# Feed-forward products transposed by VectorE blocks and DRAM transfers instead of by TensorE, with selective forcing of tasks

## The chip, the cores and the metric

One core of a Trainium2 chip runs the kernel. The metric is the device time of one execution in microseconds (us). Three timed executions of the kernel before took 2844.18, 2844.20 and 2846.04 us, so the median is 2844.2 us. The rows further down come from one more execution, taken by the hardware profiler.

## What is computed

A trunk of two blocks works on an input `x` of 256 tokens and 2048 channels in fp32. The first block has two layers, each with a mixer and a feed-forward part; the second block is a state-space and pooling layer. The part that the change touches is the feed-forward, with 5632 hidden channels:

```
def swiglu(u, w_gate, w_up, w_down):
    return (jax.nn.silu(u @ w_gate) * (u @ w_up)) @ w_down

def first_block(x, ...):
    h = x
    for layer in range(DEPTH):                       # 2
        u = rms_norm(h, mix_norm_pre[layer])
        u = even_mixer(u, ...) if layer % 2 == 0 else odd_mixer(u, ...)
        h = h + rms_norm(u, mix_norm_post[layer])
        u = swiglu(rms_norm(h, ffn_norm_pre[layer]), w_gate, w_up, w_down)
        h = h + rms_norm(u, ffn_norm_post[layer])
    return h
```

## The kernel before

Every large product runs as **units**. A unit is one block of 128 rows of a weight matrix by 512 of its columns, for both halves (t = 0, 1) of the 256 tokens. To hold fp32 accuracy each operand is split into a high and a low part, so a unit is six matmuls: `wh` by `uh`, `wl` by `uh` and `wh` by `ul` (L329 to L331), twice. A **panel** is 512 output columns, in the feed-forward's gate and up products 16 units long.

Weights come in **chunks** of two units. `fetch` (L225) issues a 512 KB transfer per chunk into `wr` on SyncE's queue (SP), which has five buffers. `split` then lets ScalarE (ACT) write `wh` and VectorE (DVE) write `wl` (L363 and L364) into four buffers each, three chunks ahead of TensorE (PE).

The Python program writes the instructions of all engines in one order by hand, and each engine works through its own instructions in that order. `order` lays out the units; between units it hangs in **hooks** (norms, transposes of `h`) and **tasks**. A task is a generator: each `yield n` lets n units pass before its next step, and `tick`, after every unit, steps at most three tasks that are due. `drain(sel)` forces the tasks in `sel` to their end at one spot. In doing so it steps every task that is alive, whether it is in `sel` or not.

One drain stands at unit 15 of the first product: it forces the first norm (`rms`) because the product's result needs its factor `rs`. Alive at that spot are also `load_gains(1, ...)`, which issues five small transfers to `gsrc`, yields 30 units, and then transposes `gsrc` on PE (L157); and `ab_proj`, which loads `abw` and yields 7.

In the feed-forward (`ffn`) the 11 pairs of gate and up panels come in three parts of 4, 4 and 3, each followed by the down product over that part's columns. `gate_evac` makes `sg`, and `up_evac` multiplies it with the up result into `mid` (L483), one 128x512 tile for each t. The down product needs `mid` with hidden channels on the partitions, so a task, four or five units later, transposes it on PE in four 128x128 pieces (`transposes`, L467) into the PSUM tile `aux`, and ACT and DVE split that into `mh` and `ml` (L360 and L361). A drain at unit 10 of the down product (unit 6 in the last part) sees to it that this has been issued. The down product runs four panels, each over all 16 (or 12) K blocks in order. Layer 0's feed-forward also carries the task `ssm_prep`, which prepares tables of the second block with DVE work and transfers of its own.

Of the kernel before, what the change touches and what calls it, by code (L numbers as in the profile page):

```python
# [10 lines left out]
F32 = mybir.dt.float32  # L11
# [4 lines left out]
OP = mybir.AluOpType  # L16
# [4 lines left out]
P = 128  # L21
# [76 lines left out]
def trunk(ctx: ExitStack, tc: tile.TileContext, I, out):  # L98
    nc = tc.nc
    PE, ACT, DVE, POOL = nc.tensor, nc.scalar, nc.vector, nc.gpsimd  # L100
# [9 lines left out]
    drp = ctx.enter_context(tc.tile_pool(name="drp", bufs=1, space=DRAM))  # L110
# [4 lines left out]
    def big(name, dt=F32R):  # L115
        return bp.tile([P, KT, S], dt, name=name, tag="b16")

    def aux(name="aux"):
        return psa.tile([P, 512], F32, name=name, tag="aux")

    def t4(name, n=1024, dt=F32):
        return t4p.tile([P, 1024], dt, name=name, tag="t4")[:, :n]

    def t2(name, n=512, dt=F32):
        return t2p.tile([P, 512], dt, name=name, tag="t2")[:, :n]
# [34 lines left out]
    units, chunks, tasks, now = [], [], [], [0]  # L160
    phs, due = [], []

    def phase(norm=True, begin=None):
        phs.append(dict(a=len(units), norm=norm, begin=begin))

    def gemm(src, wap, kts, panels, evac, kc=2, gi=None, late=None):

        steps = [(j, 0, len(kts)) for j in range(len(panels))]
        if late:
            steps[:2] = [(0, 0, late), (1, 0, late), (0, late, len(kts)), (1, late, len(kts))]  # L170
        pss = [{} for _ in panels]
        for j, g0, g1 in steps:
            c0, c1 = panels[j]
            n = c1 - c0
            for g in range(g0, g1, kc):
                ks = kts[g:g + kc]
                chunks.append((wap, ks, c0, c1, gi))
                for i, k in enumerate(ks):
                    units.append(dict(chunk=len(chunks) - 1, i=i, k=k, src=src, n=n, j=j, pn=pss[j],
                                      first=g + i == 0, last=g + i == len(kts) - 1, evac=evac,  # L180
                                      before=[], after=[]))

    def spawn(gen, gap=3, delay=1):
        tasks.append(Task(gen, gap, now[0] + delay))
        return tasks[-1]
# [15 lines left out]
        due.append((now[0] + n, f))  # L201

    def drain(sel):
        while any(not x.done for x in sel):
            for d in due:
                d[1]()
            due.clear()
            moved = [x.step(now[0]) for x in list(tasks)]
            tasks[:] = [x for x in tasks if not x.done]
            assert any(moved)  # L210

    W, nf = {}, [0]
    LA, SA, HEAD, TAIL, EXTRA, CAP = 4, 3, 12, 8, 3, 3
# [37 lines left out]
    def order():  # L251
# [3 lines left out]
        for pi, (p, end) in enumerate(zip(phs, ends)):  # L255
# [19 lines left out]
            if nm.norm:  # L275
                us[KT - 1]["before"].append(lambda n=nm: drain([n.task]))
# [72 lines left out]
    def square_sum(src, ss, t, j):  # L349
        junk = sp.tile([P, 512], BF16, name="junk", tag="junk", bufs=1)  # L350
        ACT.activation(junk[:, :src.shape[-1]], src, AF.Square, accum_out=ss[:, t, j:j + 1])  # L351
# [4 lines left out]
    st = dict(upd=lambda t, c: None, post=lambda t: None)  # L356

    def split_evac(hi, lo, src, gain=None):
        if gain is None:
            ACT.activation(hi, src, AF.Copy)  # L360
            DVE.tensor_sub(lo, src, hi.bitcast(F32))  # L361
        else:
            ACT.activation(hi, src, AF.Copy, scale=gain)  # L363
            DVE.scalar_tensor_tensor(lo, src, gain, hi.bitcast(F32), OP.mult, OP.subtract)  # L364
# [56 lines left out]
    def cut(x, j):  # L421
        return x[j // 2][:, (j % 2) * 512:(j % 2 + 1) * 512]
# [21 lines left out]
    def cols(n, base=0, w=512):  # L444
        return [(base + i * w, base + (i + 1) * w) for i in range(n)]
# [13 lines left out]
    def h_src(k):  # L459
        a, b = st["mh"][k // 8]  # L460
        return a[:, k % 8, :], b[:, k % 8, :]

    def transposes(src):

        p4 = aux()
        for i in range(4):
            PE.transpose(p4[:, i * P:(i + 1) * P], src[:, i * P:(i + 1) * P], ident)  # L467
        return p4

    def ffn(layer, gi, begin=None, end=None):  # L470
        phase(begin=begin)
        wg, wu, wd = I["ffn_w_gate"][layer], I["ffn_w_up"][layer], I["ffn_w_down"][layer]
        sg = {}

        def gate_evac(j, t, src):
            s = t2("sg")
            ACT.activation(s, src, AF.Silu, scale=st["rs"][:, t:t + 1])
            sg[t] = s

        def up_evac(p0):  # L480
            def f(j, t, src):
                m = t2("mid")
                DVE.scalar_tensor_tensor(m, src, st["rs"][:, t:t + 1], sg[t], OP.mult, OP.mult)  # L483
                mh, ml = st["m"]

                def go():
                    p4 = transposes(m)
                    k = p0 * 4
                    v = p4.rearrange("p (k s) -> p k s", k=4)
                    split_evac(mh[:, k:k + 4, t * P:(t + 1) * P], ml[:, k:k + 4, t * P:(t + 1) * P], v)  # L490
                    yield
                st["mid_tasks"].append(spawn(go(), delay=4 + t))
            return f

        def down_evac(first, last):
            def f(j, t, src):
                acc = cut(st["acc"][t], j)
                if first:
                    ACT.activation(acc, src, AF.Copy)
                    return  # L500
                DVE.tensor_add(acc, src, acc)
                if last:
                    square_sum(acc, st["ssp"], t, j)
                    if j < 3:
                        POOL.tensor_mul(acc, acc, cut(st["wpost"], j))  # L505
                    elif t == 0:
                        post_end(True)
            return f

        for pi, (p0, p1) in enumerate(PARTS):  # L510
            b = len(units)
            for p in range(p0, p1):
                gemm(u_src, wg, KTS, [(p * 512, (p + 1) * 512)], gate_evac, gi=gi)
                gemm(u_src, wu, KTS, [(p * 512, (p + 1) * 512)], up_evac(p - p0), gi=gi)
            units[b]["before"].append(lambda: st.update(m=(big("mh"), big("ml")), mid_tasks=[]))
            c = len(units)
            kts = list(range((p1 - p0) * 4))
            gemm(m_src, wd[p0 * 512:p1 * 512, :], kts, cols(4), down_evac(pi == 0, pi == 2))
            units[c + len(kts) - 6]["before"].append(lambda: drain(st["mid_tasks"]))
            if pi == 0:  # L520
                units[c]["before"].append(post_begin)
            if pi == 2:
                units[c]["before"].append(lambda: load_post(I["ffn_norm_post"][layer]))
            if pi == 2 and end:
                units[c]["before"].append(end)
# [1072 lines left out]

    mix0()
    ffn(0, 1, prep, lambda: drain([ssm["task"]]))  # L1600
    mix1()
    ffn(1, 3)
# [28 lines left out]
```

## Time and profile before

| what | value |
|---|---|
| median of three timed executions | 2844.2 us |
| the profiled execution | 2845.48 us |
| its span, first to last instruction | 2843.7 us |
| mean granted clock of TensorE | 0.996 |
| busy share PE, DVE, ACT, GpSimd (POOL) | 99%, 62%, 53%, 7% |
| moved by DMA | 552.25 MB, mean 194 GB/s |

An engine's busy share counts the time in which at least one of its instructions runs. Matmuls overlap (each takes some 0.39 us, while one starts every 0.23 us), so PE's real pace is read from the starts of its instructions. PEld is PE's weight load, which overlaps its matmuls. Idle time is put down to what ended it.

### The profile page before, as it was taken

To read this page: it belongs to the slowest core of one execution; us is meant where nothing else is said; L and a number is where in the kernel's file an instruction comes from. 1 tells how busy PE (TensorE), PEld (TensorE's weight loads), DVE (VectorE), ACT (ScalarE), POOL (GpSimd) and SP (SyncE) were. 2 spreads that over 40 slices of the span, in tenths; PEclk is the share of its full clock that TensorE was granted. 3 is DMA by queue.
4 is the path that set the end of the run, shared out by engine and by line. 5 is a ranking of instruction groups with operands and counts; after the bars stand their busy time and mean duration, and the time that the engine had idled before them with its cause. 6 is when DMAs were issued, how large, how long until landed. Compare 5 with 4: busy or idle time off the path is not lost.

```text
span 2843.7 us, 36948 instructions
## 1 busy us (share of the span) xinstructions
PE 2812.8 (99%) x13599; PEld 2312.8 (81%) x13599; DVE 1771.2 (62%) x2703; ACT 1504.9 (53%) x2380; POOL 192.6 (7%) x290
## 2 busy tenths in 40 slices
PE   7999999999999999999999999999999999999998
PEld 5888888888888778878888888888888887878887
DVE  4777766678666666566666565545555556575555
ACT  4666554655555445555555465545544545555444
POOL 0150410000000011000000000000000001100000
PEclk9999999999999999999999999999999999999999
DMA  6564746576767677755556656666656665875654
GB/s 204 170 183 139 196 151 198 162 209 204 219 212 210 213 212 235 228 172 182 171 170 186 190 179 192 188 193 191 190 191 191 189 207 185 298 249 177 194 192 144
DMA packets 305670, 552.25 MB, mean 194 GB/s; under 512 B 43032, under 2 KB 52816, under 8 KB 305488
## 3 DMA queue, kind: packets, MB, share of 16 engines
q1 hardware_dynamic: 295232, 515.52, 59.8%
q0 software_dynamic: 10224, 34.35, 3.8%
q8 instruction: 107, 1.75, 0.3%
q14 instruction: 75, 0.61, 0.1%
q10 hardware_dynamic: 32, 0.01, 0.0%
HBM read 532.24 MB, written 21.76 MB: 195 GB/s over the span
## 4 chain that ended last, share of the span: by engine, by line
PE 95%; DVE 2%; DMA 1%; ACT 1%; issue 0%; SPq 0%; ACTq 0%; POOLq 0%; POOL 0%; DVEq 0%
PE mm L329 30%; PE mm L331 29%; PE mm L330 29%; PE aux L467 1%; DVE wl L364 1%; PE aux L380 1%; ACT wh L363 0%; PE aux L1359 0%; DMA wr<-in_ev_w_in_dram 0%; DMA wr<-in_ffn_w_up_dram 0%; DMA b<-in_b_im_dram 0%; PE aux L1449 0%; PE aux L1218 0%; PE aux L556 0%; PE aux L582 0%
## 5 line engine op out<-in xcount | busy, mean ns | idle before, releaser
L364 DVE SCALAR_TENSOR_TENSOR wl<-wr,gT,wh 128x512 fp32r<-128x512 f32 x1248 | 884.6, 752 | 545.9 <-ACT wh L363 544.7
L363 ACT ACTIVATE wh<-wr,gT 128x512 fp32r<-128x512 f32 x1248 | 829.8, 716 | 536.8 <-PE mm L331 495.9
L329 PE MATMUL mm<-wh,uh 128*128 128x512 f32 (+1 forms) x2656 | 1058.5, 399 | 2.6 <-ACT uh L360 1.3
L331 PE MATMUL mm<-wh,ul 128*128 128x512 f32 (+1 forms) x2656 | 1032.5, 389 | 1.6 <-DVE ul L361 1.6
L330 PE MATMUL mm<-wl,uh 128*128 128x512 f32 (+1 forms) x2656 | 1030.2, 388 | 1.1 <-DVE wl L242 0.9
L242 DVE TENSOR_TENSOR wl<-wr,wh 128x1024 fp32r<-128x1024 f32 x324 | 401.3, 1243 | 355.6 <-ACT wh L241 355.2
L331 PEld LDWEIGHTS mm<-wh,ul 128*128 128x128 f32 x2656 | 499.6, 188 | 111.0 <-DVE ul L361 6.9
L329 PEld LDWEIGHTS mm<-wh,uh 128*128 128x128 f32 x2656 | 500.4, 188 | 104.8 <-issue 5.7
L330 PEld LDWEIGHTS mm<-wl,uh 128*128 128x128 f32 x2656 | 500.9, 189 | 97.5 <-DVE wl L364 2.1
L241 ACT ACTIVATE wh<-wr 128x1024 fp32r<-128x1024 f32 x324 | 342.5, 1059 | 398.9 <-PE mm L331 389.8
L329 PE MATMUL mm<-wh,mh 128*128 128x512 f32 x832 | 326.7, 393 | 0.0
L331 PE MATMUL mm<-wh,ml 128*128 128x512 f32 x832 | 324.0, 389 | 0.0
L330 PE MATMUL mm<-wl,mh 128*128 128x512 f32 x832 | 323.8, 389 | 0.0
L329 PEld LDWEIGHTS mm<-wh,mh 128*128 128x128 f32 x832 | 156.2, 188 | 32.8 <-issue 1.4
L331 PEld LDWEIGHTS mm<-wh,ml 128*128 128x128 f32 x832 | 156.2, 188 | 32.7
L330 PEld LDWEIGHTS mm<-wl,mh 128*128 128x128 f32 x832 | 156.3, 188 | 31.5
L505 POOL TENSOR_TENSOR acc<-acc,wpost 128x512 f32<-128x512 f32 x12 | 15.3, 1300 | 789.5 <-ACT junk L351 789.5
L360 ACT ACTIVATE uh<-aux 128x512 fp32r<-128x512 f32 x48 | 28.6, 595 | 63.5 <-PE aux L380 63.5
L360 ACT ACTIVATE mh<-aux 128x512 fp32r<-128x512 f32 (+1 forms) x60 | 32.5, 542 | 55.4 <-PE aux L467 39.1
L361 DVE TENSOR_TENSOR ul<-aux,uh 128x512 fp32r<-128x512 f32 x48 | 32.7, 689 | 41.0 <-ACT uh L360 40.8
L361 DVE TENSOR_TENSOR ml<-aux,mh 128x512 fp32r<-128x512 f32 (+1 forms) x60 | 37.1, 619 | 32.9 <-ACT mh L360 32.1
L347 POOL TENSOR_TENSOR rp<-ms,half 128x1 f32<-128x1 f32 x8 | 6.7, 840 | 471.8 <-DVE ms L346 471.8
(445 smaller groups left out, 2033.1 us busy)
## 6 DMA issues: line engine op xcount, KB each, us to landing
wr<-in_ffn_w_gate_dram SPq DMA_DIRECT2D x176, 512.0 KB, 4.4
wr<-in_ffn_w_up_dram SPq DMA_DIRECT2D x176, 512.0 KB, 4.2
wr<-in_ffn_w_down_dram SPq DMA_DIRECT2D x176, 512.0 KB, 4.5
wr<-in_ev_w_in_dram SPq DMA_DIRECT2D x112, 512.0 KB, 3.9
wr<-in_od_w_in_dram SPq DMA_DIRECT2D x96, 512.0 KB, 3.7
wr<-in_w_in_dram SPq DMA_DIRECT2D x64, 512.0 KB, 4.9
wr<-in_ev_w_out_dram SPq DMA_DIRECT2D x32, 512.0 KB, 4.0
wr<-in_od_w_out_dram SPq DMA_DIRECT2D x32, 512.0 KB, 4.5
```

Of the source, the lines that this page charges most:

```text
L241: ACT.activation(hi, r[:, k:k + m, :], AF.Copy)
L242: DVE.tensor_sub(lo, r[:, k:k + m, :], hi.bitcast(F32))
L329: PE.matmul(o, a, wh, start=u["first"], stop=False)
L330: PE.matmul(o, a, wl, start=False, stop=False)
L331: PE.matmul(o, b, wh, start=False, stop=u["last"])
L360: ACT.activation(hi, src, AF.Copy)
L361: DVE.tensor_sub(lo, src, hi.bitcast(F32))
L363: ACT.activation(hi, src, AF.Copy, scale=gain)
L364: DVE.scalar_tensor_tensor(lo, src, gain, hi.bitcast(F32), OP.mult, OP.subtract)
L380: PE.transpose(p4[:, i * P:(i + 1) * P], h[:, t, k * P:(k + 1) * P], ident)
L467: PE.transpose(p4[:, i * P:(i + 1) * P], src[:, i * P:(i + 1) * P], ident)
L505: POOL.tensor_mul(acc, acc, cut(st["wpost"], j))
```

## The change

Three things change.

- `drain` steps only the tasks that were asked for. The others are stepped, and things set for later are done, only if none of the asked ones can move.
- The products of both token halves go into one tile `mid` of 128x1024. One task per panel pair replaces two. It transposes 32x32 blocks with two DVE instructions into `ty` (`turn`), writes `ty` to a DRAM tile `td` with one transfer of 512 KB (`away`), reads it back into `tz` with four transfers of 128 KB, each to 32 partitions and in runs of 128 numbers, which puts the blocks into their places (`back`), and splits `tz` into `mh` and `ml`. Between these steps pass 2, 4, 5 and 1 units.
- The down product starts its first two panels without the last four K blocks: panels 0 and 1 run over the others, then both over the last four (`late`). The drains move along: all but the last task at the old spot, the last one at unit 22 (14 in the last part).

```
     def drain(sel):
+
         while any(not x.done for x in sel):
-            for d in due:
-                d[1]()
-            due.clear()
-            moved = [x.step(now[0]) for x in list(tasks)]
+            moved = [x.step(now[0]) for x in list(tasks) if x in sel]
+            if not any(moved):
+                for d in due:
+                    d[1]()
+                due.clear()
+                moved = [x.step(now[0]) for x in list(tasks)]
+                assert any(moved)
             tasks[:] = [x for x in tasks if not x.done]
-            assert any(moved)
...
+    def turn(x):
+        n, w = x.shape[1:]
+        y = t4("ty", n * w)
+        for t in range(n):
+            DVE.transpose(y[:, t * w:(t + 1) * w], x[:, t, :].rearrange("p (k b j) -> p b k j", b=4, j=32))
+        return y.rearrange("p (t x) -> p t x", t=n)
+
+    def away(y):
+        d = drp.tile([P, 2, 512], F32, name="td", tag="td", bufs=4)
+        nc.sync.dma_start(d, y)
+        return d
+
+    def back(z, d):
+        n, w = d.shape[1:]
+        for b in range(4):
+            nc.sync.dma_start(z[32 * b:32 * b + 32].rearrange("j (t a) x -> j t a x", t=n),
+                              d.rearrange("(a j) t (b x) -> j t a b x", a=4, b=4)[:, :, :, b])
...
             def f(j, t, src):
-                m = t2("mid")
-                DVE.scalar_tensor_tensor(m, src, st["rs"][:, t:t + 1], sg[t], OP.mult, OP.mult)
+                if t == 0:
+                    st["mid"] = t4("mid").rearrange("p (t c) -> p t c", t=2)
+                m = st["mid"]
+                DVE.scalar_tensor_tensor(m[:, t, :], src, st["rs"][:, t:t + 1], sg[t], OP.mult, OP.mult)
+                if t == 0:
+                    return
                 mh, ml = st["m"]
 
                 def go():
-                    p4 = transposes(m)
+                    y = turn(m)
+                    yield 2
+                    d = away(y)
+                    yield 4
+                    z = t4("tz").rearrange("p (a x) -> p a x", a=8)
+                    back(z, d)
+                    yield 5
                     k = p0 * 4
-                    v = p4.rearrange("p (k s) -> p k s", k=4)
-                    split_evac(mh[:, k:k + 4, t * P:(t + 1) * P], ml[:, k:k + 4, t * P:(t + 1) * P], v)
-                    yield
-                st["mid_tasks"].append(spawn(go(), delay=4 + t))
+                    for t in range(2):
+                        split_evac(*[x[:, k:k + 4, t * P:(t + 1) * P].rearrange("p k (a i) -> p k a i", a=4)
+                                     for x in (mh, ml)], z[:, 4 * t:4 * t + 4].rearrange("p a (k i) -> p k a i", k=4))
+                        yield 1
+                st["mid_tasks"].append(spawn(go(), delay=1))
...
-            gemm(m_src, wd[p0 * 512:p1 * 512, :], kts, cols(4), down_evac(pi == 0, pi == 2))
-            units[c + len(kts) - 6]["before"].append(lambda: drain(st["mid_tasks"]))
+            gemm(m_src, wd[p0 * 512:p1 * 512, :], kts, cols(4), down_evac(pi == 0, pi == 2), late=len(kts) - 4)
+            units[c + 2 * len(kts) - 10]["before"].append(lambda: drain(st["mid_tasks"]))
+            units[c + len(kts) - 6]["before"].append(lambda: drain(st["mid_tasks"][:-1]))
```

Two places show what moves. In the changed kernel the lines up to `drain` keep their numbers, those behind it stand 3 lines lower, and those behind the feed-forward 35 lines lower (L329 is now L332, L364 is L367, L1017 is L1052).

**The drain at unit 15 of the first product.** On PE, before:

```order
L330 MATMUL mm<-wl,uh 128x512
L331 MATMUL mm<-wh,ul 128x512
L157 MATMUL aux<-ident,gsrc 128x72
L329 MATMUL mm<-wh,uh 128x512
L330 MATMUL mm<-wl,uh 128x512
```

and in the changed kernel, where the transpose of `gsrc` now stands:

```order
L333 MATMUL mm<-wl,uh 128x512
L334 MATMUL mm<-wh,ul 128x512
L157 MATMUL aux<-ident,gsrc 128x72
L772 MATMUL aux<-ident,tmq 128x128 x4
L332 MATMUL mm<-wh,uh 128x512
```

The transpose stood ahead of unit 15; now it stands 31 units later, and units 15 to 45 run before it. On DVE at the same place, before:

```order
L638 MEMSET zero 128x1024
L398 TENSOR_REDUCE ms<-ssq 128x2
L399 TENSOR_SCALAR ms<-ms 128x2
L402 TENSOR_SCALAR rq<-rs 128x2
L660 TENSOR_TENSOR abw<-abw,gT 128x256
L361 TENSOR_TENSOR abs<-abw,abs 128x256
L1017 TENSOR_SCALAR tmq<-mm,rs 128x512 x2
L364 SCALAR_TENSOR_TENSOR wl<-wr,gT,wh 128x512 x6
```

and now:

```order
L673 MEMSET zero 128x1024
L401 TENSOR_REDUCE ms<-ssq 128x2
L402 TENSOR_SCALAR ms<-ms 128x2
L405 TENSOR_SCALAR rq<-rs 128x2
L1052 TENSOR_SCALAR tmq<-mm,rs 128x512 x2
L367 SCALAR_TENSOR_TENSOR wl<-wr,gT,wh 128x512 x8
L695 TENSOR_TENSOR abw<-abw,gT 128x256
L364 TENSOR_TENSOR abs<-abw,abs 128x256
```

The work on `abw`, which waits for a transfer, moved behind the evacuation of the first panel (`tmq`) and eight splits of weights.

**The second panel pair of layer 1's feed-forward.** On SP, before:

```order
L225 DMA wr<-in_ffn_w_gate_dram 128x2x512 x8
L225 DMA wr<-in_ffn_w_up_dram 128x2x512 x8
L225 DMA wr<-in_ffn_w_gate_dram 128x2x512 x8
L225 DMA wr<-in_ffn_w_up_dram 128x2x512 x8
L225 DMA wr<-in_ffn_w_gate_dram 128x2x512 x8
```

and now:

```order
L228 DMA wr<-in_ffn_w_gate_dram 128x2x512 x8
L476 DMA td<-ty 128x1024
L228 DMA wr<-in_ffn_w_up_dram 128x2x512 x2
L483 DMA tz<-td 32x8x128 x4
L228 DMA wr<-in_ffn_w_up_dram 128x2x512 x6
```

The product of the pair just finished leaves behind the next gate panel's eight weight transfers and comes back two weight transfers later, with six behind it. On ACT at the same place, before:

```order
L477 ACTIVATE sg<-mm,rs 128x512 x2
L363 ACTIVATE wh<-wr,gT 128x512 x20
L360 ACTIVATE mh<-aux 128x4x128 x2
L363 ACTIVATE wh<-wr,gT 128x512 x12
L477 ACTIVATE sg<-mm,rs 128x512 x2
```

and now:

```order
L500 ACTIVATE sg<-mm,rs 128x512 x2
L366 ACTIVATE wh<-wr,gT 128x512 x28
L363 ACTIVATE mh<-tz 128x4x128 x2
L366 ACTIVATE wh<-wr,gT 128x512 x4
L500 ACTIVATE sg<-mm,rs 128x512 x2
```

The split of the product moved back by eight weight splits, which is four chunks.

## Rows read from the trace of the kernel before

**Rows 1.** The page: busy time (us), share of span, instructions of each engine.

```profile
PE 2812.8 (99%) x13599; PEld 2312.8 (81%) x13599; DVE 1771.2 (62%) x2703; ACT 1504.9 (53%) x2380; POOL 192.6 (7%) x290
```

**Rows 2.** Waits of PE, longest first: us in total, times, longest.

```profile
PE aux L157 <- DMA gsrc<-in_norm_gain_dram: 10.6, 1, 10.6
...
PE aux L467 <- DVE mid L483: 0.6, 1, 0.6
```

**Rows 3.** Timeline of ACT in layer 1: start, us, instruction [idle before <-releaser].

```profile
1749.75 1.34 ACT L363 ACTIVATE wh<-wr,gT 128x512 fp32r<-128x512 f32 x2 [1.38 <-PE mm L331]
```

**Rows 4.** Timeline of PE, layer 1: plain matmuls, then around one transposed product.

```profile
1729.80 0.39 PE L330 MATMUL mm<-wl,uh 128*128 128x512 f32 x1
...
1732.29 0.39 PE L329 MATMUL mm<-wh,uh 128*128 128x512 f32 x1
...
1738.87 0.39 PE L331 MATMUL mm<-wh,ul 128*128 128x512 f32 x1
1739.10 0.60 PE L467 MATMUL aux<-ident,mid 128*128 128x128 f32 x4
...
1740.69 0.39 PE L331 MATMUL mm<-wh,ul 128*128 128x512 f32 x1
```

**Rows 5.** Line L467: its transposes of `mid`, ns min/median/max, first and last start.

```profile
L467 PE MATMUL aux<-ident,mid x176: 270/272/327, 551.5 to 2315.5; 128*128 128x128 f32 x176
```

**Rows 6.** Timeline of PE around the drain at unit 15.

```profile
35.18 0.39 PE L331 MATMUL mm<-wh,ul 128*128 128x512 f32 x1
46.20 0.35 PE L157 MATMUL aux<-ident,gsrc 72*128 72x72 f32 x1 [10.64 <-DMA gsrc<-in_norm_gain_dram]
46.30 0.77 PE L329 MATMUL mm<-wh,uh 128*128 128x512 f32 x1
...
51.57 0.56 PE L329 MATMUL mm<-wh,uh 128*128 128x512 f32 x1
```

**Rows 7.** Busy us by stretch: PE, PEld, DVE, ACT, POOL, then clock, DMA share, GB/s.

```profile
46.20:52.00 5.80, 5.79 (x15) 4.57 (x16) 3.68 (x6) 1.98 (x4) 0.00 (x0) 0.51 0.59 180
```

**Rows 8.** Timeline of DVE behind the drain at unit 15.

```profile
36.15 1.41 DVE L364 SCALAR_TENSOR_TENSOR wl<-wr,gT,wh 128x512 fp32r<-128x512 f32 x2 [1.18 <-ACT wh L363]
...
41.95 0.17 DVE L402 TENSOR_SCALAR rq<-rs 128x2 f32<-128x2 f32 x1 [2.94 <-POOL rs L400]
47.04 0.42 DVE L660 TENSOR_TENSOR abw<-abw,gT 128x256 f32<-128x256 f32 x1 [4.92 <-DMA abw<-in_ev_w_in_dram]
```

**Rows 9.** Groups of DVE: line, operation, count | busy us, mean ns | idle before.

```profile
L242 DVE TENSOR_TENSOR wl<-wr,wh 128x1024 fp32r<-128x1024 f32 x324 | 401.3, 1243 | 355.6 <-ACT wh L241 355.2
...
L483 DVE SCALAR_TENSOR_TENSOR mid<-mm,rs,sg 128x512 f32<-128x512 f32 x44 | 30.9, 744 | 0.0
```

**Rows 10.** Timeline of DVE and of SP at the end of that panel.

```profile
1734.58 1.41 DVE L483 SCALAR_TENSOR_TENSOR mid<-mm,rs,sg 128x512 f32<-128x512 f32 x2
...
1737.42 20.35 SPq L225 DMA_DIRECT2D wr<-in_ffn_w_up_dram  x8
```

**Rows 11.** DMA issues: count, KB each, median us from issue to landing.

```profile
wr<-in_ffn_w_up_dram SPq DMA_DIRECT2D x176, 512.0 KB, 4.2
...
ms<-M POOLq DMA_DIRECT2D x2, 512.0 KB, 4.5
```

**Rows 12.** Line L885, the transfers `mb<-ms`, which fill 32 partitions each: landing.

```profile
DMA to landing us min/median/max: 3.2/4.4/5.9
```

**Rows 13.** Layer 0's first pairs: the chain (start, us, piece), ACT, PE, DVE stretch.

```profile
560.62 0.58 SPq L1049
...
563.84 7.51 DMA b<-in_b_im_dram
...
580.25 5.40 ACT L363 ACTIVATE wh<-wr,gT 128x512 fp32r<-128x512 f32 x8 [7.56 <-DMA wr<-in_ffn_w_up_dram]
...
581.81 0.50 PE L330 MATMUL mm<-wl,uh 128*128 128x512 f32 x1
...
620.00:640.00 20.00, 20.00 (x90) 16.57 (x89) 19.27 (x58) 9.96 (x15) 0.00 (x0) 1.00 0.65 185
```

## The prediction

> **What bounds the kernel now.** I read the page's busy times, then the waits of the busy engine, then the timeline of what feeds it. PE is busy 99% of the span [rows 1], which alone says little, since matmuls overlap. The waits say more: PE's largest is one of 10.6 us, and the changed lines have one more, of 0.6 us [rows 2]. Third, who waits for whom in the long steady stretches: ACT, which splits the weights for PE, sits idle 1.38 us before every pair of splits until PE frees a buffer [rows 3]. So the feeders wait for PE and not the other way round, and a microsecond of instructions taken off PE's queue is a microsecond off the end.
>
> I sum against the profiled execution, span 2843.7 us, 2845.5 us in all; that lies 1.3 us above the median of 2844.2, and savings carry over unchanged.
>
> **Transposes off PE (gain 20.2).** Undisturbed, eleven matmul starts take 1732.29 - 1729.80 = 2.49 us, 0.2264 each. Across a group of four transposes, six matmuls further on, 1740.69 - 1738.87 = 1.82 us pass where 6 x 0.2264 = 1.36 would [rows 4], so a group costs 0.46 us of PE's stream. There are 176 transposes [rows 5], 44 groups: 44 x 0.46 = 20.2 us. The 0.6 us in which PE waited for `mid` [rows 2] goes with them, since PE no longer reads `mid`.
>
> **Forcing only the asked task (gain 13.2).** At unit 15 the old drain also pushed `load_gains` past its 30 units of waiting, so PE's transpose of `gsrc` stood in front of unit 15 and waited 10.64 us for a transfer that had just been issued [rows 6]. After that idle stretch the granted clock was 0.51 [rows 7], half of 2.4 GHz: from 46.30 to 51.57 twelve matmul starts took 5.27 us and not 12 x 0.2264 = 2.72 [rows 6], another 2.55. In the new order 31 units stand ahead of that transpose, and the sum is 10.64 + 2.55 = 13.2.
>
> What is late next there? Eleven chunks are split by then (the last pair of `wl` at 36.15 [rows 8]), which is units 0 to 21. PE, free from 35.4, eats units 15 to 21 in 7 x 6 x 0.2264 = 9.5 us, until 44.9. DVE's next splits now stand behind `rq` (41.95, it waits for POOL [rows 8]) and two `tmq` (0.74 each, the price of `mid`, the same kind of PSUM read [rows 9]): they start at 43.6 and the first is done at 44.4. I cost this at nothing, with half a microsecond of cover; each microsecond that `rq` is later is one lost. `abw`, landed at 47.04 [rows 8], comes behind eight splits and no longer holds them up.
>
> **The round trip (costed at nothing in the steady stretches).** No row shows a DVE transpose. Below, a 128x512 pass over SBUF costs 1243 / 2 = 620 ns, and `mid` 744 [rows 9]; I take 0.74, as an instruction on the same tile, and 1.5 as the far end. Per pair: `mid` runs 1734.58 to 1735.99 [rows 10], `ty` is ready at 1737.5. SP is then just at its next weight transfer (1737.42 [rows 10]), so `td` leaves at once. The nearest row for writing 512 KB to DRAM lands after 4.5 us [rows 11]: 1742.0. Four issues of some 0.6 us each (as SP's small loads, 560.62 [rows 13]) and a landing of 3.2 to 5.9 us, as other transfers into 32 partitions take [rows 12], bring `tz` by 1749.7 at the latest. ACT reaches the split of `mh` behind four more chunks, that is behind the pair at 1749.75 [rows 3], which runs 0.9 earlier without the two groups of transposes: at 1750.2. So ACT barely waits.
>
> Three queues are passed. On ACT and DVE the weight splits stand behind the split of `tz`. Four `wh` buffers hold three chunks ahead of PE, 3 x 2.72 = 8.2 us (a chunk is 12 matmuls), of which a split by ACT and DVE needs 2.1; so ACT may be held for some 6 us before PE feels it. On SP weight transfers stand behind the wait for `td` and the four issues. The third of them is due at 1737.42 + 2 x 2.72 = 1742.9 and leaves at 1744.4, 1.5 us late. A weight transfer lands in 4.2 us [rows 11] and ACT wants it 11 us after its issue (five buffers), so this is hidden. DVE gains 44 x 0.74 = 33 us over the two feed-forwards; it is 62% busy [rows 1], and where it is fullest, 19.27 of 20 us [rows 13], the same buffers cover the delay.
>
> The down product now wants the last pair's K blocks at its unit 24, 24 x 1.36 = 32.6 us after the panel's end (21.7 in the last parts); the trip needs 1750.2 + 2.1 - 1734.4 = 18. In the old order they would be wanted at unit 12, after 16.3, so moving them back is what hides the trip.
>
> *A rule against this.* The Trainium skill, "VectorE: DVE Perf Modes", section "Rules for kernel authors", gives 128x128 transposes to TensorE when PSUM may hold the result, as it may here, because VectorE turns only 32x32 blocks. The row agrees that PE's way is short, 0.46 us against a trip of 15. By the rule the sum would be a loss; by the rows it is a gain, because PE's queue is the one that ends last and the trip stands beside it.
>
> **Layer 0's first pairs (loss 2.4).** Here there is no slack. `ssm_prep`'s loads of `b` hold the queue until the next weights land at 580, ACT waits 7.56 us for them, and PE just notices: its start at 581.81 is late by a tenth of a microsecond [rows 13]. The 0.9 us saved on the first pair's two groups is given back there, since PE only waits longer. `td` and `tz` go out just ahead of those loads. If all their landing time came on top it would be 4.5 + 5.9 = 10.4 us; if they are through before, as SP's issue times suggest (550 to 557, the loads from 563.84), nothing. I take 1.5, near the lower end. Sum: 0.9 + 1.5 = 2.4.
>
> In the mixer of layer 0 the selective drain shifts the first group's tasks by 8 units; PE's other instructions keep their places, so I cost it at nothing.
>
> **Sum.** 20.2 + 0.6 + 13.2 - 2.4 = 31.6. The span becomes 2812.1 and the median 2844.2 - 31.6 = 2812.6 us.
>
> **Rivals.**
>
> *The round trip ends on the path (slower).* ACT works in order: while it waits for `tz`, weight splits wait behind it. This decides once `tz` lands over 6 us after 1750, 19 us after `td` left, where I count 12. Each further microsecond costs 22, one per pair; at 1.4 the gain is gone, at 3 the time is 2812.6 + 66 = 2879. For it: no row shows this pattern of transfer, and the queue is shared with 194 GB/s of weights. Against: both nearest rows lie well below [rows 11, 12]. 5%. The Trainium skill, "VectorE: DVE Perf Modes", section "The three transpose paths", warns that a plain copy which transposes by strides is 19 times slower than the crossbar when the innermost destination stride is large. That would be this rival; here runs of 128 numbers stay whole on both sides, and only `turn` reorders within them.
>
> *The wait for `gsrc` is replaced by one for weights.* If POOL brings `rs` some microseconds later, or splits are late, PE idles after unit 21 and the clock may fall again: 5 to 13 of the 13.2 are lost, 2818 to 2826. 9%.
>
> *The first pairs lose all 10.4.* 2812.6 + 8.9 = 2821.5. 11%.
>
> *PE's stream was not the bound.* If splits set the pace, the transposes filled holes, and only the 13.2 remain: 2831. ACT's idle time speaks against it [rows 3]. 4%.
>
> *Several small losses, 1.2 us per pair,* from ACT waiting while its buffers are not yet full again: 2839 to 2850, about no change. 3%.
>
> **How the numbers follow.** 68% stay for the forecast, 2806 to 2819: the lower end if the first pairs lose nothing (2810) and some of PE's small remaining waits go with the new order. With most of the second and third rival, 2806 to 2824 holds some 84%. About 0.2% (5.7 us) is what a measurement of this kernel can tell from no change. Faster: 68 + 9 + 11 + 4 = 92%. Same 3%, slower 5%.
>
> **What would show it.** PE: no L467 on `mid`, no wait for `gsrc`, the clock at 1.00 from the start-up on, 0.2264 between matmuls through every feed-forward. DVE: a transpose of 0.6 to 1.5 us. SP and ACT: `td` landing in some 4.5 us, `tz` in under 6, ACT idle for `tz` under 2 us a pair. A wait of PE for `wl` or `wh` some 12 units into each panel would mean the first rival; one near 45 us the second; one of over 4 us near 580 the third.

## The result, and the profile after

The changed kernel took 2814.68 us (median of four runs, 2812.86 to 2815.96) beside 2844.38 for the kernel before: a ratio of 0.9895, 95% interval 0.988 to 0.9909, 29.7 us less. The forecast was 2812.6 within 2806 to 2824. In a second series beside other kernels it took 2812.55 (2812.17 to 2813.25), ratio 0.9889 (0.9875 to 0.9902), so some 2 us of difference between series must be allowed for. The profiled execution took 2812.86 us, span 2811.0 after 2843.7, 32.7 us less.

Where the 32.7 us went can be read off by unit, since both programs run the same 1912 units in stretches of the same length. The table holds the start of the first matmul of a unit in the two traces, in us (counted by six matmuls a unit, since at the ends of a large product the two token halves run one after the other).

```
unit   what ends there                  before     after   after - before   change
  12   start-up                          30.88     31.20       +0.32
 160   drain, first part of mixer 0     298.34    287.15      -11.19        -11.51
 288   mixer 0                          499.92    488.73      -11.19          0.00
 816   feed-forward of layer 0         1253.48   1230.99      -22.49        -11.30
1072   mixer 1                         1643.11   1620.64      -22.47         +0.02
1600   feed-forward of layer 1         2376.11   2343.35      -32.76        -10.29
1880   most of the second block        2809.98   2776.67      -33.31         -0.55
```

So there are two gains, the drain's and the transposes'. Behind unit 1880 the changed kernel gives 0.66 us back, which leaves 32.65. The first gain, 11.5, is smaller than the 10.64 us of idle time and 2.55 us of slow clock that went with the wait for `gsrc`. The page's busy times, the waits of PE and its state in the stretch of [rows 7], in the changed kernel:

```profile
PE 2789.5 (99%) x13423; PEld 2293.7 (82%) x13423; DVE 1790.3 (64%) x2747; ACT 1502.3 (53%) x2380; POOL 189.7 (7%) x290
```

```profile
PE aux L157 <- DMA ident<-in_cst_dram: 2.9, 1, 2.9
...
PE aux L758 <- DVE gl L754: 1.2, 2, 0.8
```

```profile
46.20:52.00 5.80, 5.80 (x27) 4.77 (x26) 3.71 (x7) 1.31 (x3) 0.00 (x0) 1.00 0.93 236
```

PE has 176 instructions fewer, the transposes. Its wait of 10.6 us and the one for `mid` [rows 2] are gone (the 2.9 us for `ident`, at the start, are in both kernels), and the granted clock is 1.00, the 2.4 GHz level, where it was 0.51. A small new wait has come, for `gl` in the mixer.

The handover after unit 21, for which the prediction counted half a microsecond of cover. PE first:

```profile
44.36 0.39 PE L334 MATMUL mm<-wh,ul 128*128 128x512 f32 x1
44.59 0.39 PE L332 MATMUL mm<-wh,uh 128*128 128x512 f32 x1
...
45.27 0.39 PE L332 MATMUL mm<-wh,uh 128*128 128x512 f32 x1
```

and DVE:

```profile
42.28 0.17 DVE L405 TENSOR_SCALAR rq<-rs 128x2 f32<-128x2 f32 x1 [2.95 <-POOL rs L403]
42.36 1.40 DVE L1052 TENSOR_SCALAR tmq<-mm,rs 128x512 f32<-128x512 f32 x2
43.68 5.38 DVE L367 SCALAR_TENSOR_TENSOR wl<-wr,gT,wh 128x512 fp32r<-128x512 f32 x8
49.33 0.43 DVE L695 TENSOR_TENSOR abw<-abw,gT 128x256 f32<-128x256 f32 x1 [0.27 <-DMA abw<-in_ev_w_in_dram]
```

The splits start at 43.68, so the first is done at 44.4; PE starts unit 22 at 45.27 and finds it. The matmuls there start every 0.23 us without a break.

The round trip, by the lines of the blocks (L471), the write (L476) and the read-back (L483): count, ns min/median/max, first and last start, and landing.

```profile
L471 DVE STREAM_TRANSPOSE ty<-mid x44: 664/685/707, 537.1 to 2279.1; 128x512 f32<-128x512 f32 x44
```

```profile
L476 SPq DMA_DIRECT2D td<-ty x22: 326/339/1925, 538.4 to 2279.8; - x22
...
DMA to landing us min/median/max: 2.7/3.5/7.0
```

```profile
L483 SPq DMA_DIRECT2D tz<-td x88: 562/606/1433, 541.7 to 2288.7; - x88
...
  ACT mh L363: 9.7, 7
...
DMA to landing us min/median/max: 3.2/5.6/6.6
```

From the end of `ty` to the last landing of `tz` that is 10.6 to 15.0 us per pair, mostly 11 to 12. ACT waited for it 9.7 us in all, in 7 places, six of them in layer 0 (at most 3.1 us, at its second pair), and 0.4 us at layer 1's last pair. The Trainium skill, "DMA: Bandwidth & Descriptors", section "Anatomy of one DMA — SWDGE (gpsimd) path", fits a transfer by about 2.0 us and its bytes at 436 GB/s; for the 512 KB of `td` that makes an estimate of 3.2 us, and the trace shows 3.5 in the median and up to 7.0, though on SyncE's hardware queue.

### The profile page after: what moved, and what is told of

The parts are those of the page before. It is cut to its first block, busy times and chain, and to the rows that moved or that the text cites. A ratio compares the mean times of both kernels' runs of the same rounds, so it can differ in the third digit from the quotient of the medians.

```text
span 2811.0 us, 36863 instructions
## 1 busy us (share of the span) xinstructions
PE 2789.5 (99%) x13423; PEld 2293.7 (82%) x13423; DVE 1790.3 (64%) x2747; ACT 1502.3 (53%) x2380; POOL 189.7 (7%) x290
## 4 chain that ended last, share of the span: by engine, by line
PE 97%; DVE 2%; ACT 1%; issue 0%; DMA 0%; SPq 0%; ACTq 0%; POOLq 0%; POOL 0%; DVEq 0%
PE mm L332 30%; PE mm L334 30%; PE mm L333 30%; DVE wl L367 1%; PE aux L490 1%; PE aux L383 1%; DMA wr<-in_ev_w_in_dram 0%; PE aux L1394 0%; PE aux L1484 0%; PE aux L1253 0%; PE aux L591 0%; PE aux L617 0%; DVE ul L364 0%; PE aux L1309 0%; PE aux L703 0%
## 5 line engine op out<-in xcount | busy, mean ns | idle before, releaser
L367 DVE SCALAR_TENSOR_TENSOR wl<-wr,gT,wh 128x512 fp32r<-128x512 f32 x1248 | 880.0, 749 | 526.8 <-ACT wh L366 524.6
L332 PE MATMUL mm<-wh,uh 128*128 128x512 f32 (+1 forms) x2656 | 1055.0, 397 | 2.7 <-ACT uh L363 1.4
L332 PEld LDWEIGHTS mm<-wh,uh 128*128 128x128 f32 x2656 | 499.6, 188 | 105.9 <-issue 5.5
L332 PE MATMUL mm<-wh,mh 128*128 128x512 f32 x832 | 325.6, 391 | 0.0
L332 PEld LDWEIGHTS mm<-wh,mh 128*128 128x128 f32 x832 | 156.2, 188 | 33.2 <-issue 1.4
L334 PEld LDWEIGHTS mm<-wh,ml 128*128 128x128 f32 x832 | 156.1, 188 | 32.7
L333 PEld LDWEIGHTS mm<-wl,mh 128*128 128x128 f32 x832 | 156.2, 188 | 31.8
L364 DVE TENSOR_TENSOR ul<-aux,uh 128x512 fp32r<-128x512 f32 x48 | 32.7, 688 | 40.8 <-ACT uh L363 40.6
L354 ACT ACTIVATE junk<-h 128x512 bf16<-128x512 f32 (+1 forms) x50 | 30.5, 610 | 14.6 <-DVE h L1582 13.8
L500 ACT ACTIVATE sg<-mm,rs 128x512 f32<-128x512 f32 x44 | 29.8, 689 | 13.7 <-PE mm L334 13.7
```

Source lines behind the costliest of these rows:

```text
L332: PE.matmul(o, a, wh, start=u["first"], stop=False)
L333: PE.matmul(o, a, wl, start=False, stop=False)
L334: PE.matmul(o, b, wh, start=False, stop=u["last"])
```

## The experiments

There are eleven runs, one of them (e4) of the changed kernel itself. Differences between stretches are again those of unit starts, against the profiled execution of the changed kernel. The first four ran together.

### One part alone, and the drain in between

e1 is the kernel before with the new `drain` only; e2 is the changed kernel with the old one; e3 forces `ab_proj` too, but not `load_gains`:

```
-            moved = [x.step(now[0]) for x in list(tasks) if x in sel]
+            moved = [x.step(now[0]) for x in list(tasks) if x in sel or x in forced]
...
             done.append(spawn(ab_proj()))
+            forced.append(done[-1])
```

> The kernel before with the selective drain alone; the products are still transposed by TensorE. My theory (three separate effects that add up: the drain's stall and slow clock, a loss in layer 0's mixer because its first group's tasks stand 8 units later, and the transposes) expects 14.4 us gained between units 15 and 30, 2.9 us lost between units 30 and 160, nothing in the feed-forwards: 2844.4 - 11.5 = 2832.9 us, range 2831 to 2835. Rival A, that the mixer's loss belongs to something else (SyncE's queue, run to run): 2830.0. Rival B, that the wait is replaced by another one for weights: over 2836.

Measured: 2833.94 us (2833.02 to 2834.89), 10.5 less than before; from unit 12 to unit 160 the trace shows 256.1 us, 11.3 less than before.

> The changed kernel with the old drain, which again steps every living task. My theory expects the stall of 10.6 us for gsrc and the slow clock behind it to be back, no loss in layer 0's mixer, and the whole gain of the transposes: 22 pairs x 0.94 = 20.6 and 0.9 in the first pair, together 21.5, so 2844.4 - 21.5 = 2822.9 us, range 2821 to 2825. A rival, that the two parts help each other or share a gain: more than 1.5 us away from that, so that the two parts alone do not add up to the change.

Measured: 2823.06 us (2822.11 to 2825.09), 21.3 less than before. The wait for `gsrc` is back with 10.5 us. In the six microseconds behind it the granted clock was 0.75, where it was 0.52 in the kernel before, and from unit 12 to 160 e2 took 266.1 us, 1.3 less than the kernel before: what the same wait costs is not the same each time.

> The changed kernel itself once more, unchanged, as the base for the others and because its four runs spread from 2812.9 to 2816.0 us while the profiled one gained 32.6 us and the median 29.7. Theory: the spread is a start-up or mixer wait that differs from run to run by 1 to 3 us, the feed-forwards agree to 0.1 us. Median expected at 2814.0, range 2812.5 to 2815.5.

Measured: 2812.55 us, 31.85 less than before. The two parts alone give 10.5 + 21.3 = 31.8: they add up, to within the microsecond or two by which such series differ. The difference from the first series is more than what any stretch of these traces shows, so it stays unexplained.

> The changed kernel, whose drain at unit 15 steps the asked task and also the one that prepares abw, as before, but still not load_gains. The tasks of the mixer's first group stand where they stood before, so by my theory the mixer's loss of 2.9 us goes. But VectorE now waits for abw (until 47 us) with weight splits behind it, and TensorE has split weights only until about 45 us: some 3 to 6 us are lost there, at half clock for a part. Net against the changed kernel 0 to +4 us, 2814.5 to 2819. The rival, that waiting for abw costs nothing since the buffers cover it: 2811.8.

Measured: 2818.59 us (2816.88 to 2820.28), 6.0 more than the changed kernel. Forcing `abw` costs more than it brings, and not through the weights, as I had written, but through PE's own products with `abs`, which stand at unit 19 again and wait. Waits of PE in e3:

```profile
PE aux L706 <- ACT abs L365: 5.3, 1, 5.3
```

Behind it the clock was lower again:

```profile
47.00:54.00 7.00, 7.00 (x45) 5.03 (x43) 3.77 (x6) 1.80 (x3) 0.00 (x0) 0.69 0.73 221
```

But the wait for `gl` is gone from e3, and the stretch from unit 30 to unit 160 takes 221.3 us, as in the kernel before (221.2), where the changed kernel needs 224.6 (in part since `abs`'s products, which stood ahead of unit 30, now stand behind it). So the small loss in the mixer comes with the place of the first group's tasks, and a part of it can be seen. In the changed kernel PE reaches the product with `gl` when DVE, which runs in order, has just begun to make it:

```profile
180.48 0.99 DVE L754 TENSOR_SCALAR gl<-cm,glog 128x128 f32<-128x128 f32 x4
```

```profile
181.62 1.10 PE L758 MATMUL aux<-gl,cm 128*128 128x512 f32 x2 [0.82 <-DVE gl L754]
```

That asked for a version with the old places and without the wait.

### abw loaded earlier and prepared in a gap

e8 is the changed kernel, in which `abw` is loaded ahead of the other small transfers and its two DVE instructions are forced, once, between `ms` and `rq`:

```
+            st["abw"] = t2("abw", S).rearrange("p (k n) -> p k n", n=16)
+            nc.sync.dma_start(st["abw"], win[:, 7168:7184].rearrange("(k p) n -> p k n", p=P))
...
-            moved = [x.step(now[0]) for x in list(tasks) if x in sel]
+            moved = [x.step(now[0]) for x in list(tasks) if x in sel or x in forced]
+            forced.clear()
```

> The changed kernel with the small weights abw loaded ahead of the other small transfers, and prepared on VectorE in the 3 us in which it waits for POOL's rs; the mixer's first group then stands where it stood before the change, with no wait for abw. My theory expects the loss of 2.9 us between units 30 and 160 to be gone, with nothing lost at unit 19: 2812.5 - 2.8 = 2809.7 us, range 2808.5 to 2811.5. The rival (the loss moves to another place of the mixer, or the early transfer holds up weights): 2812 or more.

Measured: 2810.31 us (2810.16 to 2811.03), ratio to before 0.9879 (0.9865 to 0.9892), within the range expected and the lowest median of this study. DVE of e8 at the place:

```profile
38.29 0.17 DVE L405 TENSOR_SCALAR ms<-ms 128x2 f32<-128x2 f32 x1
38.37 0.42 DVE L699 TENSOR_TENSOR abw<-abw,gT 128x256 f32<-128x256 f32 x1
39.27 0.43 DVE L367 TENSOR_TENSOR abs<-abw,abs 128x256 fp32r<-128x256 f32 x1 [0.48 <-ACT abs L366]
41.40 0.17 DVE L408 TENSOR_SCALAR rq<-rs 128x2 f32<-128x2 f32 x1 [1.71 <-POOL rs L406]
```

The preparation fills the time in which DVE waits for POOL. From unit 12 to 160 the kernel before takes 267.5 us, the changed one 255.95 and e8 254.0. The drain is thus worth 13.5 us with the order kept, and the moved tasks cost 1.95 of it. Of these 1.95 us PE's two waits for `gl` are 1.2; e8 has neither, and no other wait of PE in that stretch differs by more than 0.2 us, so the rest is not traced to a cause. The 14.4 and 2.9 of my expectations for e1 were both too large, since the borders that I had taken cut through the moved tasks; their difference holds.

### How much waiting the round trip may cause

e5 and e6 move the split of `tz` ahead, so that ACT comes for it too early:

```
                     y = turn(m)
-                    yield 2
+                    yield 2          # e6: 1
                     d = away(y)
-                    yield 4
+                    yield 4          # e6: 1
...
-                    yield 5
+                    yield 1          # e6: 1
```

> The changed kernel with the split of the read-back product four units (5.4 us) earlier in the order of ScalarE and VectorE; the transfers leave as before. In layer 1 of the changed kernel the product lands 0.4 to 2.3 us before ScalarE reaches it, so ScalarE then waits 3 to 5 us per pair, in layer 0 up to 9. My theory (the three split chunks that lie ahead of TensorE cover about 6 us of waiting) expects no loss in layer 1 and at most a few us in layer 0's pairs: 2812.5 to 2818, likeliest 2814. The rival (every microsecond that ScalarE waits is felt by TensorE): 22 x 4 = 88 us more, 2900. A second rival (nothing can be lost up to 8 us): 2812.5.

Measured: 2838.92 us (2834.28 to 2844.16). Neither theory: 26 us are lost, all in layer 0 (27.5 us from unit 288 to 816), and 0.0 from unit 1072 to 1600. A pair of layer 0 and one of layer 1, on ACT of e5:

```profile
599.79 1.15 ACT L363 ACTIVATE mh<-tz 128x512 fp32r<-128x512 f32 x2 [10.03 <-DMA tz<-td]
...
1752.20 1.15 ACT L363 ACTIVATE mh<-tz 128x512 fp32r<-128x512 f32 x2 [4.16 <-DMA tz<-td]
```

In layer 1 ACT waits 3.3 to 4.7 us a pair, 6.1 in the last, and PE feels none of it. In layer 0 it waits 3.6 to 10.0, and more than half of PE's idle time there (5.3 + 2.2 + 1.7 + 1.2 = 10.4 of 18.3 us) stands before small products of `ssm_prep` (L1253, L1270, L1309) and not before weights. By the time lost the two are about even: 14.9 us go in the first part, where ACT waits up to 10.0 us and PE idles for weights alone (7.9 us, with the slow clock behind them), and 12.6 in the other two, where it idles for the small products (10.4). Waits of PE in e5, 560 to 1250 us:

```profile
PE aux L1309 <- DVE cpo L1304: 5.3, 2, 3.1
PE mm L332 <- ACT wh L366: 2.3, 1, 2.3
PE aux L1309 <- ACT wh L244: 2.2, 1, 2.2
PE mm L332 <- ACT wh L244: 2.0, 1, 2.0
PE mm L333 <- DVE wl L245: 2.0, 2, 1.8
PE aux L1270 <- DMA cs<-in_c_im_dram: 1.7, 1, 1.7
PE mm L333 <- DVE wl L367: 1.6, 3, 0.7
PE aux L1253 <- DVE bt L1246: 1.2, 1, 1.2
```

> The changed kernel with all steps of the round trip one unit apart, so the split stands eight units (10.9 us) earlier, the transfers at most a microsecond earlier in fact, and SyncE holds the weight transfers behind its wait for the write. ScalarE then waits 9 to 11 us per pair. My theory (6 us are covered, each further microsecond costs one, per pair) expects PE to lose 3 to 5 us in each of 22 pairs, and some more at the lower clock: 2880 to 2925. The rival (the trip can be hidden whole by other buffers): below 2830. The rival (all waiting is felt): 22 x 10 = 220, about 3030.

Measured: 2862.77 us (2856.89 to 2863.57), less than I expected, since the trip is shorter when the read-back leaves before the next weights: 7.3 to 9.1 us in layer 1, 10.7 in its last pair. ACT waited 5.8 to 7.2 us a pair there, 9.1 in the last, and the feed-forward of layer 1 lost 4.1 us in all. By unit starts, pairs with a wait up to 6.5 us lost at most 0.1, the two with 7.2 and 7.1 lost 0.4 and 0.9, the last one 2.8. So the weight buffers cover some 6.5 us, as the prediction counted (some 6). Layer 0 lost 46.5. Two pairs of layer 1, on ACT of e6:

```profile
1726.10 1.16 ACT L363 ACTIVATE mh<-tz 128x512 fp32r<-128x512 f32 x2 [7.16 <-DMA tz<-td]
...
1769.33 1.15 ACT L363 ACTIVATE mh<-tz 128x512 fp32r<-128x512 f32 x2 [6.46 <-DMA tz<-td]
```

e10 is e5 with `ssm_prep` moved into the other feed-forward:

```
-    ffn(0, 1, prep, lambda: drain([ssm["task"]]))
+    ffn(0, 1)
     mix1()
-    ffn(1, 3)
+    ffn(1, 3, prep, lambda: drain([ssm["task"]]))
```

> The kernel of e5 (split four units earlier, 26 us lost, by the trace all of it in layer 0's feed-forward) with ssm_prep moved from layer 0's feed-forward into layer 1's. My theory now (the round trip's cover is short only where ssm_prep's own work stands behind the same wait and where its transfers lengthen the trip; the weight buffers alone cover the 4 us) expects the loss to move with it: layer 0's feed-forward loses at most 2 us against the changed kernel, layer 1's 20 to 30, in all 2832 to 2846. The rival (the loss belongs to layer 0 or to the first feed-forward as such, or to all transfers): layer 0 still loses over 10 us.

Measured: 2835.28 us (2832.17 to 2842.09). The loss moved with it. Layer 0's feed-forward took 722.7 us from unit 288 to 816, the same as layer 1's in the changed kernel (722.7 from 1072 to 1600), although ACT waited 3.4 to 4.8 us in every pair. Layer 1's took 39.7 us more than in the changed kernel, of which 742.3 - 722.7 = 19.6 are `ssm_prep`'s own share by the difference of the changed kernel's two feed-forwards; 20.1 were lost. PE's waits in e10, 500 to 1260 us and then 1660 to 2400:

```profile
PE mm L334 <- DVE ul L364: 0.7, 2, 0.4
PE aux L383 <- DVE h L444: 0.2, 1, 0.2
```

```profile
PE aux L1309 <- DVE cpo L1304: 6.0, 2, 3.4
PE mm L333 <- DVE wl L367: 2.0, 5, 0.6
```

So what limits the trip is not the layer and not the transfers of weights but `ssm_prep`. Two ways show in the changed kernel too. DVE is behind in three of layer 0's pairs, the second to the fourth, so that `mid` starts 2.8 to 4.2 us after the start of the panel's last matmul and the trip starts late. Layer 0's third pair, whose last matmul starts at 623.72, on DVE and in its stretch:

```profile
623.95 0.28 DVE L1175 TENSOR_TENSOR prg<-pw,prg 128x64 f32<-128x64 f32 x1
...
626.73 1.41 DVE L508 SCALAR_TENSOR_TENSOR mid<-mm,rs,sg 128x512 f32<-128x512 f32 x2
```

```profile
620.00:640.00 20.00, 20.00 (x90) 16.57 (x89) 19.52 (x47) 9.41 (x15) 0.00 (x0) 1.00 0.82 233
```

And the product with `cpo` follows the DVE work that makes its operand by only three units (4.1 us) in the order, less than the weight buffers cover. That is how one trip in the changed kernel already touches PE: at unit 591, where `td` takes 7.0 us to land behind small transfers of `ssm_prep` and the trip is 15 us long, ACT waits 1.5 us for `tz`, and PE's product with `cpo` came 0.15 us late, in e4 0.7, in e3 1.8 (against the usual time between these instructions).

e9 is e8 with the split two units later (`yield 7` for `yield 5`), to give those pairs room.

> The kernel of e8 with the split of the product two units (2.7 us) later in the order. In the changed kernel ScalarE waits 1.5 to 3.8 us for the product in layer 0's pairs, and TensorE loses 0.2 to 0.7 us (once 1.8) at unit 591, where its small product for ssm_prep stands behind that wait. My theory expects these to go and nothing else to move: 2810.3 - 0.5 = 2809.8 us, range 2809 to 2810.6. The rival (the later split makes the down product wait for the last pair, wanted 21.7 us after the panel's end in the last parts and then ready after some 20.7): 2811.5 or more.

Measured: 2810.91 us (2810.28 to 2811.16), 0.3 us above the range that I gave and not told apart from e8. The stall at unit 591 (1.05 us in e8) is gone from the trace, but what that brings is within the spread of the runs. The down product did not wait.

### The moved K blocks

e7 leaves out `late` and forces the last pair at the old spot:

```
-            gemm(m_src, wd[p0 * 512:p1 * 512, :], kts, cols(4), down_evac(pi == 0, pi == 2), late=len(kts) - 4)
-            units[c + 2 * len(kts) - 10]["before"].append(lambda: drain(st["mid_tasks"]))
-            units[c + len(kts) - 6]["before"].append(lambda: drain(st["mid_tasks"][:-1]))
+            gemm(m_src, wd[p0 * 512:p1 * 512, :], kts, cols(4), down_evac(pi == 0, pi == 2))
+            units[c + len(kts) - 6]["before"].append(lambda: drain(st["mid_tasks"]))
```

> The changed kernel without the moved K blocks: the down product runs its panels in the old order, and the split of the last pair is forced at the old spot. The last pair's product is wanted at unit 12 of the down product (16.3 us after the panel's end), in the last part at unit 8 (10.9 us); a trip of 11.5 us after 3 us for the products and blocks plus two splits is ready after 16.5. My theory expects next to nothing in the four parts of 16 blocks (0 to 1 us each), 5 to 6 us in each of the two parts of 12, with some at the lower clock: 2812.5 + 13 = 2826, range 2820 to 2832. The rival (moving the K blocks is of no use, the buffers cover that too): 2812.5.

Measured: 2832.42 us (2827.99 to 2836.71), 19.9 more than the changed kernel and just above my range; its profiled execution, the fastest of the four, has 15.1 more in its span, and only these can be placed. By stretches: 2.7, 0.3 and 7.2 us in layer 0's three parts, 0.0, 0.0 and 5.3 in layer 1's. PE's wait in the last part of layer 0 and its clock behind it:

```profile
1182.96 0.80 PE L332 MATMUL mm<-wh,mh 128*128 128x512 f32 x1 [4.22 <-ACT mh L363]
```

```profile
1183.00:1189.00 6.00, 6.00 (x15) 4.70 (x16) 3.60 (x4) 2.84 (x4) 0.00 (x0) 0.52 0.35 101
```

A wait of 4.2 us cost 7.2, since fifteen matmuls went through in 6 us at a clock of 0.52 where 28 do at 1.00. In the last part of layer 1 a wait of 3.5 us cost 5.3. Moving the blocks back is needed, and most of it, 12.5 of the 15.5 us, in the parts of twelve blocks. The 2.7 in the first part, where I had expected at most 1, stand for 2.0 in its down product, with a wait of 1.5 us for `mh`, and 0.7 ahead of it.

### The loads of b between write and read-back

e11 starts `ssm_prep` six units earlier (`delay=26` for `delay=32`), so that its loads stand between `td` and `tz` of the first pair.

> The changed kernel with ssm_prep started six units earlier, so that its loads of b stand on SyncE's queue between the write and the read-back of the first pair's product, the place of which the prediction was afraid. The prediction's bound for that (all landing time comes on top) gives 9 to 10 us lost, 2822. My theory now: the read-back leaves some 9 us later, ScalarE waits 6 to 10 us for it, and the buffers cover most of that; but the weights behind it are late as well, so TensorE loses 1 to 5 us: 2813.5 to 2818, likeliest 2815.5. If nothing is lost (2812.5), the place was never a danger.

Measured: 2820.34 us (2819.85 to 2821.23), 7.8 more than the changed kernel, 7.0 of it in the first part of layer 0. SP of e11, and ACT:

```profile
537.60 0.34 SPq L476 DMA_DIRECT2D td<-ty  x1
...
543.10 0.66 SPq L1091 DMA_DIRECT2D b<-in_b_re_dram  x1
...
555.49 2.60 SPq L483 DMA_DIRECT2D tz<-td  x4
```

```profile
562.24 1.15 ACT L363 ACTIVATE mh<-tz 128x512 fp32r<-128x512 f32 x2 [11.22 <-DMA tz<-td]
```

```profile
564.05 0.50 PE L332 MATMUL mm<-wh,uh 128*128 128x512 f32 x1 [3.53 <-ACT wh L366]
```

`td` leaves at 537.60, `tz` only at 555.49 behind the loads, and ACT waits 11.2 us. PE idles 3.5 us, as its line shows, so 7 to 8 were covered. It idles 0.9 more one matmul later and loses the rest of its 7 us at a clock of 0.72 behind the gap. My expectation of 1 to 5 left the clock out. The danger that the prediction priced at up to 10.4 us of landing time, 8.9 over its forecast, is real and near that size; the changed kernel escapes it because there `tz` is issued before the first load of `b`, as SP of the changed kernel shows:

```profile
541.75 2.64 SPq L483 DMA_DIRECT2D tz<-td  x4
...
551.17 0.64 SPq L1091 DMA_DIRECT2D b<-in_b_re_dram  x1
```

## Why the prediction was right, step by step

The forecast of 2812.6 lay 2.1 us below the first series and at the second. Its steps did not all hold, and that it came so close is in part luck: two errors of about 2 us cancelled, as told below.

- **Transposes off PE, 20.2 + 0.6.** Right. e2 gained 21.3; in the two traces the feed-forwards are 11.30 and 10.29 us shorter. Layer 1's eleven pairs give 10.29 / 11 = 0.94 each, two groups of 0.47, where 0.46 was read [rows 4]. Layer 0's extra microsecond is for the larger part the wait for `mid`, 0.6 [rows 2], and 0.3 lie in the kernel before's first pair, where matmuls near 582 and 585 came late. In e4 layer 0 is only 10.5 us shorter than before.
- **Forcing only the asked task, 13.2.** Right in itself: 13.5 by e8. How much of it is slow clock varies, though: e2, with the same wait, needs only 12.1 us more than e8 from unit 12 to 160. What was late next there was as worked out: `rq` at 42.28, splits at 43.68, and PE reached unit 22 at 45.27, 0.9 us after the first split.
- **The mixer's shift by eight units, nothing.** Wrong by 2.0 us. I looked whether PE's order changes and not whether tasks that make PE's operands on DVE keep their lead; two products with `gl` then waited, which is 1.2 of the 2.0.
- **The round trip, nothing in the steady stretches.** Right, with less room than stated in layer 0. A 128x512 block pass took 685 ns (0.74 taken), `td` landed after 3.5 us (4.5 taken), `tz` after 5.6 (3.2 to 5.9), the trip mostly 11 to 12 (12.2 at the latest), but up to 15.0 in layer 0, where ACT's idle time also passed the 2 us a pair named as a sign, once, with 3.1. PE lost 0.15 us by it at unit 591. The pair of layer 1 that answers to [rows 3, 10], on SP and ACT:

```profile
1713.86 0.34 SPq L476 DMA_DIRECT2D td<-ty  x1
...
1717.44 2.58 SPq L483 DMA_DIRECT2D tz<-td  x4
```

```profile
1726.69 1.14 ACT L363 ACTIVATE mh<-tz 128x512 fp32r<-128x512 f32 x2
```

  `tz` has landed at 1725.35, 1.3 us before ACT comes to it.
- **Layer 0's first pairs, a loss of 2.4.** Did not happen. `td` and `tz` were through at 550, before the loads of `b`, and ACT's long wait for weights is as it was, with PE again hardly touched (0.15 us late near 572):

```profile
551.25 1.14 ACT L363 ACTIVATE mh<-tz 128x512 fp32r<-128x512 f32 x2
...
567.80 1.34 ACT L366 ACTIVATE wh<-wr,gT 128x512 fp32r<-128x512 f32 x2 [7.23 <-DMA wr<-in_ffn_w_up_dram]
```

  The 0.9 us of the first pair's groups was kept too. This caution and the loss in the mixer, 2.4 against 2.0, cancelled, and that is luck.
- **The rival on the path, 22 us for each microsecond past some 6.** The 6 us are right for a pair whose feeders do nothing else (6.5 hidden in e6). For layer 0 the rule is wrong: there a split 5.4 us earlier already cost 26, since DVE starts the trip late in three pairs and PE's own small products for `ssm_prep` wait as well. The margin of the change is thus smaller than the prediction said, and is set by eleven of the 22 pairs.
- **A rule against it.** The Trainium skill, "VectorE: DVE Perf Modes", section "Rules for kernel authors", sends 128x128 transposes to TensorE. For the latency of one product that holds (0.47 us a group against a trip of 11); for this kernel's time the trace speaks the other way, 0.94 us gained per pair.

## What to carry to other kernels

Where one engine's queue is the bound, work may be taken off it by a way some twelve times as long (a trip of 11 us for 0.94 us of PE), if the result is wanted later than that; what must be counted is the least room among all consumers that stand behind the wait, and small side tasks have less of it than the weight buffers. When a change to a scheduler makes tasks slip, look at each task's lead over the busy engine and not at that engine's order alone. Four waits of TensorE of 3.5 to 5.3 us cost about one and a half times their idle time here, for the clock behind them (two others, of 3.1 and 3.4 us, left it at 1.00), so an order that avoids the wait altogether is worth more than one that shortens it.

## What was not expected

- The read-back of 128 KB a transfer in runs of 128 numbers (512 bytes) landed not much later than plain transfers: 5.6 us in the median for each of four queued together, 512 KB in all, beside 4.4 us of one 512 KB transfer of weights on the same queue.
- Four idle stretches of TensorE, of 3.5 us with 0.9 right behind it (e11), 4.2 and 3.5 (e7) and 5.3 (e3), were each followed by a stretch at a lower granted clock (0.72, 0.52, 0.74 and 0.69); with that they cost 7.0, 7.2, 5.3 and 7.7 us (e3 against e8, from unit 12 to 30). The length of a wait does not decide it alone: in e5 a wait of 2.3 us that ended at 601.61 was followed by six microseconds at 0.72, and one of 3.1 us that ended at 1121.90 by 1.00, as was one of 3.4 us in e10 (2227.09). What tells them apart was not tested.
- Two series of the same kernel, on different occasions, differed by 2.1 us in the median (2814.68 and 2812.55) while each spread over 1 to 3 us; no stretch of the traces at hand accounts for it.
